# Rotary rows of layer 0's latent heads in blocks of four heads, and where modulation steps, scales and weight slots stand

## The chip, the cores and the metric

One core of one Trainium2 chip. The metric is device microseconds of one execution of the whole program, the median over runs. TensorE (PE) multiplies, VectorE (DVE), ScalarE (ACT) and GpSimd (POOL) do the rest, and SyncE (SP) issues all loads.

## The reference, cut to what matters

Two layers over 256 latent and 256 context tokens of width 1024. Layer 0 mixes tokens by eight heads of window attention with a sink and eight heads of latent attention (MLA); then come 32 experts of which each token uses two. Layer 1 mixes by differential attention, and has 32 experts of its own. All is fp32. The part that the change touches is the latent attention:

```python
q = (_rmsnorm(cq, q_norm) @ w_uq).reshape(b, n, MLA_HEADS, MLA_NOPE_DIM + MLA_ROPE_DIM)
kv = (_rmsnorm(ckv, kv_norm) @ w_ukv).reshape(b, n, MLA_HEADS, MLA_NOPE_DIM + MLA_V_DIM)
...
qr_l = _rope(qr_l, rope_b)
kr_l = _rope(kr_l, rope_b)
...
q = jnp.concatenate([qn, qr], axis=-1)
k = jnp.concatenate([kn, jnp.broadcast_to(kr, kn.shape[:-1] + (MLA_ROPE_DIM,))], axis=-1)
...
s = jnp.einsum('bqhd,bkhd->bhqk', qi, k, preferred_element_type=jnp.float32) * scale
p = jax.nn.softmax(s, axis=-1).astype(v.dtype)
```

A query of a head has 64 plain rows and 32 rotary rows; the 32 rotary rows of the key are shared by all eight heads. Only the latent tokens (the first 256) are rotated. Each layer also needs six modulation vectors, products of the conditioning vectors with a 1024 x 6144 matrix.

## The kernel before, in words

Everything is one program whose order on each engine is the order in which the code is written. A product that must keep fp32 accuracy is made of three fp32r matmuls (`mm3`, L397): each operand is split into a rounded part hi and a rest lo (`split`, L389: a cast on ScalarE at L392, a subtraction at L395 on VectorE or GpSimd), and hi x hi, hi x lo, lo x hi are summed.

Weights flow through one stream in a fixed order (`plan`, `emit`, `pump`, L172) into a pool of 24 slots of 1 MB, shared with data. `budget(n)` says how many slots are kept for data; the next load is issued on SP's queue as soon as fewer weight slots than the rest are held. The order is: input projections, latent up-projections, 19 pieces of modulation weights, four tiles of output projection, five more pieces, the experts of layer 0. Of the experts, the first four are known beforehand; the loads of the others are held back until the ranks of the experts are known (`rank_ids`, L1192, matmuls at L1196; L1199 lifts the limit).

A modulation step (`ada_step`, L317, called by `fill`, L377) multiplies one piece: four fp32 matmuls in four column groups of TensorE (L324). After the eighth step of a vector pair the result is copied (L329), and the next `fill` turns it into place (L359, L364).

Layer 0's attention goes in three stages. **Input projections:** queries, keys and values of the window heads by `mm3`, rotated by `rope_lat` (L566: a product with the cosines at L570, quarter by quarter products with the sines at L573 that swap the halves, a sum at L574); beside them the statistics of the latents, and the shared rotary key (`kr_sum`, L648: a selecting matmul at L650, then `rope_lat`). Four modulation steps lie here.

**Up-projections** (loop at L865, four head pairs): for each head a query matmul group of 128 columns, made of 64 plain rows, 32 rotary rows and zeros (L402 to L404 into psA), a copy (L874), `rope_lat` on rows 64 to 127, and a split. For each pair a key group, whose rows are copied (L890) into a 128-row buffer that holds the rotary key in its lower half (L888), and a split for each head; and a value group, copied at L895. The 16 splits are called through `late` (L657), one behind, with their subtraction on GpSimd. Two modulation steps lie here, and the scores, maxima and exponentials of the first two units (`first`, L861).

**Units** (`run_units`, L776): 24 units of two heads each, numbered as 0 to 7 window heads of latent tokens, 8 to 11 window heads of context tokens, 12 to 19 latent heads of latent tokens, 20 to 23 latent heads of context tokens. Iteration i does, on TensorE: scores of unit i+2 (L688; a mask at L692 for units 0 to 7), the products with the values of unit i-1 (L768), perhaps a modulation step, and the transposes of unit i (L746). On VectorE: the two maxima of unit i+2 (L702) and their negation (L704 with the sink, L708 without), the casts of unit i-1's result (L773, L774), reciprocal and scale of unit i+1 (L733, L737), and one of the two copies of unit i's transposes (L751). On ScalarE: the other copy (L749) and the exponentials of unit i+2 (L720). Window scores have 64 rows a head, so two heads lie in the two halves of TensorE's rows; latent scores have 128 rows a head. `early0` (L908) puts four splits of output weights, 1024 columns each, on GpSimd in iterations 15, 17, 19 and 21.

Then come the output projection (`out_half`, L1563), the router, the ranks, and layer 0's experts.

Of the kernel before, what the change touches and what calls it, by code (L numbers as in the profile page):

```python
# [19 lines left out]
P = 128  # L20
# [22 lines left out]
for _n, _w in (("cosA", 256), ("sinA", 256), ("cosB", 256), ("sinB", 256), ("m0", 128), ("m1", 128), ("U", 128),  # L43
               ("sel", 128)):
    CN[_n] = (_o, _o + _w)
    _o += _w
NCN = _o
NS = 24
KU = 2
# [67 lines left out]
def model_kernel(ctx: ExitStack, tc: tile.TileContext, xin, small, cst, ada0, adaw, win, wuq, wukv, wout0, dwin,  # L117
# [467 lines left out]
    budget(20)  # L585
# [8 lines left out]
    krT = Y.v[:, 3, :]  # L594
    X = S((4, NTOK), F32R)
    Z = S((4, NTOK), F32R)

# [49 lines left out]

    def kr_sum():  # L648
        ps = psB()
        PE.matmul(ps, csv("sel"), krs, start=True, stop=True)  # L650
        ACT.copy(Y.v[64:P, 3, :], ps[64:P, :])
        rope_lat(Y.v[:, 3, :], Y.v[:, 3, :], 64, "cosB", "sinB")
# [19 lines left out]
    def unit_scores(u):  # L672
# [3 lines left out]
        for n in range(1 if lat else 2):  # L676
            q = slice(qt * P, (qt + 1) * P) if lat else slice(SEQ + n * P, SEQ + (n + 1) * P)
            ks = slice(0 if lat else SEQ, NTOK)
            for a, b in ((0, 0), (0, 1), (1, 0)):
                for i in range(2):  # L680
# [3 lines left out]
                    else:  # L684
                        h = 2 * j + i
                        ql, kl = qT[a][h // 4].v[:, h % 4, q], kT[b][h // 4].v[:, h % 4, ks]
                    o = ps[i] if lat else ps[i][:, n * SEQ:(n + 1) * SEQ]
                    PE.matmul(o, ql, kl, start=(a + b == 0), stop=(a == 1 and not masked))  # L688
# [38 lines left out]
    def unit_scale(u, res):  # L727
# [6 lines left out]
        for i in range(2):  # L734
            for n in range(nq):
                w = slice(n * (NTOK // nq), (n + 1) * (NTOK // nq))
                DVE.tensor_scalar(pts[i][:, w], pts[i][:, w], st[:, 0, i, n:n + 1], None, op0=ALU.mult)  # L737
# [107 lines left out]

    wq, wkv = W0.get(), W0.get(False)
    qT = [[S((4, NTOK), F32R) for _ in range(2)] for _ in range(2)]
    kT = [[S((4, NTOK), F32R) for _ in range(2)] for _ in range(2)]
# [10 lines left out]
    kU, ex0 = [], {}  # L859
# [5 lines left out]
    for hp in range(4):  # L865
        for i in range(2):
            h = 2 * hp + i
            if h in (6,99):
                first((6,99).index(h))
            ps = psA()  # L870
            s = slice(h * P, (h + 1) * P)
            mm3(ps, 2, lambda k: (wq[0][:, k, s], wq[1][:, k, s]), lambda k: (X.v[:, k, :], X.v[:, 2 + k, :]))
            dst = U()
            ACT.copy(dst, ps)  # L874
            rope_lat(dst, dst, 64, "cosB", "sinB")
            late(*(x[h // 4].v[:, h % 4, :] for x in qT), dst)
        if hp == 0:
            av_turn()
        if hp in (1,3):
            fill()  # L880
        ps = psB()
        s = slice(hp * P, (hp + 1) * P)
        mm3(ps, 1, lambda k: (wkv[0][:, k, s], wkv[1][:, k, s]), lambda k: kvn3)
        for i in range(2):
            h = 2 * hp + i
            if h < KU:
                kU.append(U())
                DVE.tensor_copy(kU[h][64:P, :], krT[64:P, :])  # L888
            dst = kU[h % KU]
            ACT.copy(dst[0:64, :], ps[64 * i:64 * i + 64, :])  # L890
            late(*(x[h // 4].v[:, h % 4, :] for x in kT), dst)
        ps = psB()
        s = slice(hp * P, (hp + 1) * P)
        mm3(ps, 1, lambda k: (kvn3[0][:, s], kvn3[1][:, s]), lambda k: (wkv[0][:, 0, 512:], wkv[1][:, 0, 512:]))
        DVE.tensor_copy(mv[:, hp, :], ps)  # L895
    split(*lates.pop(0), GP)
    for i in range(2):
        if i not in ex0:
            first(i)
    free(5)  # L900

    oT = [[S((KC, SEQ), F32R) for _ in range(2)]]
    budget(19)
# [4 lines left out]
    def early0(i):  # L908
        if i == 7:
            oT.append([S((KC, SEQ), F32R) for _ in range(2)])  # L910
        if i == 13:
            free(4)
            budget(19)
# [3 lines left out]
    run_units(units, unit_scores, unit_max, unit_exp, unit_scale, unit_transpose, unit_pv, lambda i: True, early0, ex=ex0)  # L917
    fill_all()
    free(9)
# [977 lines left out]
def _constants():  # L1897
# [9 lines left out]
    z = np.zeros((16, SEQ), np.float32)  # L1907
    put("cosB", np.concatenate([z, z, z, z, c.T, z, c.T, z], 0))
    put("sinB", np.concatenate([z, z, z, z, s.T, z, -s.T, z], 0))
# [102 lines left out]
```

## Time and profile before

| | |
|---|---|
| runs | 1484.48, 1480.60, 1483.35 us; median 1483.35 |
| profiled execution | 1484.73 us, its span 1482.6 us |
| TensorE, share of the span | 88% busy, weight loads 49% |
| VectorE, ScalarE, GpSimd | 41%, 26%, 9% |
| DMA | 487 MB, 329 GB/s over the span |

The page cuts the span in 40 slices of 37 us; a digit is a busy share in tenths. In a timeline a row is one instruction or a run of like ones: start, duration of the run, engine, line, operation, output <- input with shapes, count, and in brackets the idle time before it with what ended it. Matmuls overlap, so that the distance from start to start tells what they cost.

### The profile page before, as it was taken

The page shows a single profiled execution, that of the slowest core. Times are in us where ns is not written, and L with a number is a line of the kernel's source. Part 1 is how long each engine was busy: PE and PEld are TensorE (multiplying, and loading weights), DVE is VectorE, ACT ScalarE, POOL GpSimd, SP SyncE. Part 2 cuts the span into 40 slices and gives each one's busy share as a digit, 9 for nine tenths or more (in the row PEclk, how much of TensorE's full clock was granted, in tenths as well). Part 3 has the DMA queues.
Part 4 walks back from the last instruction along what each step waited for, and adds up shares of the span by engine and source line. Part 5 has one row for each costly group of instructions (what it writes and reads, how often), then busy time and mean ns, then how long its engine had stood idle before and what let it go on. Part 6 is the DMA issues. An engine that isn't in the chain of part 4 may idle for free.

```text
span 1482.6 us, 21587 instructions
## 1 busy us (share of the span) xinstructions
PE 1304.1 (88%) x8341; PEld 724.3 (49%) x8341; DVE 602.1 (41%) x1476; ACT 384.5 (26%) x819; POOL 128.0 (9%) x110
## 2 busy tenths in 40 slices
PE   6996999989999999989878999888998787788856
PEld 4673667955445343525326897584442231323313
DVE  4488896453322322222227756944321110111102
ACT  4445655331111110101115333643110010101002
POOL 1134011220000000000013111301000000000000
PEclk9998999999999999999999999999999999998999
DMA  9634715279999999999999228357999999999995
GB/s 382 266 114 152 273 48 211 90 307 374 399 420 422 421 421 420 421 422 420 408 412 382 86 86 304 135 219 276 422 420 422 421 421 420 422 421 421 421 412 228
DMA packets 70075, 487.08 MB, mean 329 GB/s; under 512 B 7632, under 2 KB 7760, under 8 KB 13392
## 3 DMA queue, kind: packets, MB, share of 16 engines
q1 hardware_dynamic: 69968, 485.65, 80.7%
q8 instruction: 68, 1.11, 0.3%
q14 instruction: 39, 0.32, 0.1%
HBM read 484.57 MB, written 1.05 MB: 328 GB/s over the span
## 4 chain that ended last, share of the span: by engine, by line
DMA 25%; PE 16%; DVE 6%; ACT 2%; issue 1%; DVEq 0%; SPq 0%; ACTq 0%
DMA s<-in_ew_dram 25%; PE psA L1336 3%; PE psA L1368 3%; PE psB L403 2%; PE psB L404 2%; PE psB L402 2%; DVE t L1728 1%; DVE u L1746 1%; DVE s L395 1%; PE psA L402 1%; PE psA L403 1%; PE psA L404 1%; PE psB L1385 1%; DVE u L573 0%; DVE s L1378 0%
## 5 line engine op out<-in xcount | busy, mean ns | idle before, releaser
L1336 PE MATMUL psA<-s 128*32 128x512 f32 (+2 forms) x2336 | 418.3, 621 | 81.4 <-DMA s<-in_ew_dram 71.6
L1336 PEld LDWEIGHTS psA<-s 128*32 128x32 f32 (+2 forms) x2336 | 113.7, 122 | 362.7 <-issue 206.2
L1378 DVE SCALAR_TENSOR_TENSOR s<-psB,modT,s 128x256 f32<-128x256 f32 x296 | 120.4, 476 | 215.6 <-PE psB L1385 215.5
L1368 PE MATMUL psA<-s,u 128*32 128x512 f32 (+1 forms) x1168 | 185.9, 601 | 12.8 <-DMA s<-in_ew_dram 11.4
L1373 DVE SCALAR_TENSOR_TENSOR u<-psA,t,u 128x512 fp32r<-128x512 f32 x48 | 36.0, 751 | 233.0 <-ACT u L1372 233.0
L1368 PEld LDWEIGHTS psA<-s,u 128*32 128x32 f32 (+1 forms) x1168 | 53.6, 119 | 123.7 <-issue 95.4
L1510 DVE TENSOR_TENSOR u<-u,psA 128x512 f32<-128x512 f32 x24 | 16.5, 688 | 224.3 <-PE psA L1336 224.3
L1385 PE MATMUL psB<-u 128*128 128x512 f32 (+1 forms) x384 | 95.8, 369 | 13.1 <-DVE s L1378 4.6
L1362 ACT COPY u<-psB 128x512 f32<-128x512 f32 x24 | 14.1, 587 | 332.6 <-PE psB L1360 332.6
L402 PE MATMUL psB<-s 128*128 128x256 f32 (+1 forms) x296 | 96.0, 324 | 3.9 <-DVE s L895 3.9
L403 PE MATMUL psB<-s 128*128 128x256 f32 (+1 forms) x296 | 95.2, 322 | 0.4 <-DVE s L395 0.4
L404 PE MATMUL psB<-s 128*128 128x256 f32 (+1 forms) x296 | 95.1, 321 | 0.0
L1385 PEld LDWEIGHTS psB<-u 128*128 128x128 f32 x384 | 58.7, 188 | 72.1 <-issue 35.7
L1372 ACT ACTIVATE u<-psA,t 128x512 fp32r<-128x512 f32 x48 | 33.0, 688 | 177.2 <-PE psA L1368 171.6
L1507 ACT ACTIVATE u<-psA 128x512 f32<-128x512 f32 x24 | 14.4, 600 | 220.8 <-PE psA L1336 220.8
L1319 PE MATMUL psB<-s 128*128 128x256 f32 x544 | 68.0, 285 | 0.7 <-ACT u L1362 0.7
L395 DVE TENSOR_TENSOR s<-s 128x1024 fp32r<-128x1024 f32 (+3 forms) x56 | 51.6, 967 | 39.9 <-ACT s L392 39.8
L1319 PEld LDWEIGHTS psB<-s 128*128 128x128 f32 x544 | 65.9, 191 | 2.6 <-issue 1.6
L402 PEld LDWEIGHTS psB<-s 128*128 128x128 f32 x296 | 56.4, 190 | 13.8 <-DVE s L895 4.8
L402 PE MATMUL psA<-s 128*128 128x256 f32 (+1 forms) x208 | 62.6, 301 | 0.0
L403 PE MATMUL psA<-s 128*128 128x256 f32 (+1 forms) x208 | 60.5, 291 | 0.0
L404 PE MATMUL psA<-s 128*128 128x256 f32 (+1 forms) x208 | 60.4, 291 | 0.0
(349 smaller groups left out, 1736.6 us busy)
## 6 DMA issues: line engine op xcount, KB each, us to landing
s<-in_ew_dram SPq DMA_DIRECT2D x376, 1024.0 KB, 19.8
s<-in_adaw_dram SPq DMA_DIRECT2D x40, 1024.0 KB, 7.5
s<-in_dwin_dram SPq DMA_DIRECT2D x12, 1024.0 KB, 10.3
s<-in_ada_dram SPq DMA_DIRECT2D x8, 1024.0 KB, 19.8
s<-in_wout_dram SPq DMA_DIRECT2D x8, 1024.0 KB, 7.7
s<-in_ew_dram SPq DMA_DIRECT2D x16, 512.0 KB, 14.4
s<-in_win_dram SPq DMA_DIRECT2D x5, 1024.0 KB, 19.9
s<-in_xin_dram SPq DMA_DIRECT2D x2, 1024.0 KB, 8.6
```

The costliest lines, as they stand in the source:

```text
L395: eng.tensor_tensor(lo, src, hi.bitcast(F32), ALU.subtract)
L402: PE.matmul(ps, lh, rh, start=(k == 0), stop=False)
L403: PE.matmul(ps, lh, rl, start=False, stop=False)
L404: PE.matmul(ps, ll, rh, start=False, stop=(k == n - 1))
L1319: PE.matmul(ps[:, i * n:(i + 1) * n], src(t, cs_(c0 + i)), oh[:, t, 0:n], start=(t == 0 and a == 0), stop=(t == T_ - 1 and a == 1))
L1336: PE.matmul(ps[sl, :], xg(hf * 4 + k, sl), wt(m, hf)[:, k, :], start=(hf == 0 and k == 0), stop=(hf == 1 and k == 3))
L1368: PE.matmul(ps[sl, :], ht[:, k, sl], wt(2, hf)[:, k, :], start=(k == 0), stop=(k == 3))
L1372: ACT.activation(yh, ps, AF.Copy, scale=gsl)
L1373: DVE.scalar_tensor_tensor(out=yl, in0=ps, scalar=gsl, in1=yh.bitcast(F32), op0=ALU.mult, op1=ALU.subtract)
L1378: DVE.scalar_tensor_tensor(out=xc(c)[:, HALF[s]], in0=ps[:, HALF[s]], scalar=modT[:, l, 5, c, s:s + 1], in1=xc(c)[:, HALF[s]], op0=ALU.mul ...
L1385: PE.matmul(ps[:, 0:nt], ysp[a][:, cs_(q)], oht[:, 0:nt], start=(a == 0), stop=(a == 1))
L1510: TT(hm, sl, pm[1], ALU.mult)
```

## The change

The query matrix is reordered: first the 64 plain rows of all heads, two heads to a block of 128, then the rotary rows of four heads to a block, then the same rotary rows with their halves exchanged. Rotary rows are made by two matmul groups, one for each order, and three operations of 128 rows (`rope32`), without the swap of quarters. The rotary key is repeated in four row groups in the same way (`sel`, `sel2`). Plain queries and keys are split straight from PSUM, for two heads at once, the rest on VectorE (`hl_out`). Scores of a latent unit are six matmuls of 64 rows and six of 32 rows. The scale of each unit's second head moves to GpSimd. Modulation steps stand in iterations i with i % 5 in (0, 2, 4), and none in the up-projections but one after them. `budget` keeps fewer slots for data, since the latent heads need six data slots where they needed nine.

```diff
--- before.py
+++ after.py
@@ -41,12 +41,11 @@
 CN = {}
 _o = 0
 for _n, _w in (("cosA", 256), ("sinA", 256), ("cosB", 256), ("sinB", 256), ("m0", 128), ("m1", 128), ("U", 128),
-               ("sel", 128)):
+               ("sel", 128), ("sel2", 128)):
     CN[_n] = (_o, _o + _w)
     _o += _w
 NCN = _o
 NS = 24
-KU = 2
 
 ADL = 3
 
@@ -582,7 +581,7 @@
         return ps
 
 
-    budget(20)
+    budget(17)
     sqs = []
     for j in range(3):
         ACT.copy(Y.v[:, j, :], pss[j])
@@ -591,9 +590,10 @@
         sqs.append(sq)
     sqv = sqs.pop()
     free(3)
-    krT = Y.v[:, 3, :]
     X = S((4, NTOK), F32R)
     Z = S((4, NTOK), F32R)
+
+    kr = [X.v[:, n, :] for n in (0, 2)]
 
     dgs = []
 
@@ -645,11 +645,20 @@
         for s in range(2):
             ACT.activation(krs[:, HALF[s]], pk[:, HALF[s]], AF.Identity, bias=krb[:, s:s + 1])
 
+    def rope32(ps, ps2, dst):
+
+        ACT.copy(dst[:, SEQ:], ps[:, SEQ:])
+        t = U((2, SEQ))
+        DVE.tensor_tensor(t[:, 0, :], ps[:, 0:SEQ], csv("cosB"), ALU.mult)
+        DVE.tensor_tensor(t[:, 1, :], ps2[:, 0:SEQ], csv("sinB"), ALU.mult)
+        DVE.tensor_tensor(dst[:, 0:SEQ], t[:, 0, :], t[:, 1, :], ALU.add)
+
     def kr_sum():
-        ps = psB()
+
+        ps, ps2 = psB(), psA()
         PE.matmul(ps, csv("sel"), krs, start=True, stop=True)
-        ACT.copy(Y.v[64:P, 3, :], ps[64:P, :])
-        rope_lat(Y.v[:, 3, :], Y.v[:, 3, :], 64, "cosB", "sinB")
+        PE.matmul(ps2[:, 0:SEQ], csv("sel2"), krs[:, 0:SEQ], start=True, stop=True)
+        rope32(ps, ps2, Y.v[:, 3, :])
 
     kvn3 = [Z.v[:, n, :] for n in (0, 3)]
     lates, nlate = [], [0]
@@ -682,10 +691,16 @@
                         pr = slice(64 * i, 64 * i + 64)
                         ql, kl = aq[a].v[pr, j, q], ak[b][pr, ks]
                     else:
-                        h = 2 * j + i
-                        ql, kl = qT[a][h // 4].v[:, h % 4, q], kT[b][h // 4].v[:, h % 4, ks]
+                        pr = slice(64 * i, 64 * i + 64)
+                        ql, kl = qn[a].v[pr, j, q], kn[b].v[pr, j, ks]
                     o = ps[i] if lat else ps[i][:, n * SEQ:(n + 1) * SEQ]
-                    PE.matmul(o, ql, kl, start=(a + b == 0), stop=(a == 1 and not masked))
+                    PE.matmul(o, ql, kl, start=(a + b == 0), stop=(a == 1 and kind == "swa" and not masked))
+            for a, b in ((0, 0), (0, 1), (1, 0)) if kind == "mla" else ():
+                for i in range(2):
+                    h = 2 * j + i
+                    pr = slice(32 * (h % 4), 32 * (h % 4) + 32)
+                    o = ps[i] if lat else ps[i][:, n * SEQ:(n + 1) * SEQ]
+                    PE.matmul(o, qr.v[pr, 2 * a + h // 4, q], kr[b][pr, ks], start=False, stop=(a == 1))
         if masked:
             b = (1 - qt) * P
             for i in range(2):
@@ -734,7 +749,11 @@
         for i in range(2):
             for n in range(nq):
                 w = slice(n * (NTOK // nq), (n + 1) * (NTOK // nq))
-                DVE.tensor_scalar(pts[i][:, w], pts[i][:, w], st[:, 0, i, n:n + 1], None, op0=ALU.mult)
+                if i:
+                    GP.tensor_tensor(pts[i][:, w], pts[i][:, w], st[:, 0, i, n:n + 1].to_broadcast([P, NTOK // nq]),
+                                     ALU.mult)
+                else:
+                    DVE.tensor_scalar(pts[i][:, w], pts[i][:, w], st[:, 0, i, n:n + 1], None, op0=ALU.mult)
         return pts
 
     def unit_transpose(u, pts):
@@ -843,9 +862,11 @@
     avt = U()
     ACT.copy(avt, ps)
 
+    split(*lates.pop(0), GP)
     wq, wkv = W0.get(), W0.get(False)
-    qT = [[S((4, NTOK), F32R) for _ in range(2)] for _ in range(2)]
-    kT = [[S((4, NTOK), F32R) for _ in range(2)] for _ in range(2)]
+    qn = [S((4, NTOK), F32R) for _ in range(2)]
+    kn = [S((4, NTOK), F32R) for _ in range(2)]
+    qr = S((4, NTOK), F32R)
     mvB = S((4, NTOK))
     mv = mvB.v
     av = Y.v[:, 0, :].rearrange("p (t n) -> p t n", t=4)
@@ -856,51 +877,50 @@
             PE.transpose(ps[:, t * P:(t + 1) * P], avt[:, t * P:(t + 1) * P], ident)
         ACT.copy(Y.v[:, 0, :], ps)
 
-    kU, ex0 = [], {}
+    ex0 = {}
 
     def first(i):
         u = units[i]
         ex0[i] = unit_exp(u, *unit_max(u, unit_scores(u)))
 
-    for hp in range(4):
-        for i in range(2):
-            h = 2 * hp + i
-            if h in (6,99):
-                first((6,99).index(h))
-            ps = psA()
-            s = slice(h * P, (h + 1) * P)
-            mm3(ps, 2, lambda k: (wq[0][:, k, s], wq[1][:, k, s]), lambda k: (X.v[:, k, :], X.v[:, 2 + k, :]))
-            dst = U()
-            ACT.copy(dst, ps)
-            rope_lat(dst, dst, 64, "cosB", "sinB")
-            late(*(x[h // 4].v[:, h % 4, :] for x in qT), dst)
-        if hp == 0:
+    def hl_out(ps, hi, lo):
+        ACT.copy(hi, ps)
+        DVE.tensor_tensor(lo, ps, hi.bitcast(F32), ALU.subtract)
+
+    def up_q(ps, blk, n):
+        s = slice(blk * P, (blk + 1) * P)
+        mm3(ps[:, 0:n], 2, lambda k: (wq[0][:, k, s], wq[1][:, k, s]),
+            lambda k: (X.v[:, k, 0:n], X.v[:, 2 + k, 0:n]))
+
+    for b in range(2):
+
+        ps, ps2 = psA(), psA()
+        up_q(ps, 4 + b, NTOK)
+        up_q(ps2, 6 + b, SEQ)
+        dst = U()
+        rope32(ps, ps2, dst)
+        split(qr.v[:, b, :], qr.v[:, 2 + b, :], dst, GP)
+        if b == 0:
             av_turn()
-        if hp in (1,3):
-            fill()
-        ps = psB()
-        s = slice(hp * P, (hp + 1) * P)
-        mm3(ps, 1, lambda k: (wkv[0][:, k, s], wkv[1][:, k, s]), lambda k: kvn3)
-        for i in range(2):
-            h = 2 * hp + i
-            if h < KU:
-                kU.append(U())
-                DVE.tensor_copy(kU[h][64:P, :], krT[64:P, :])
-            dst = kU[h % KU]
-            ACT.copy(dst[0:64, :], ps[64 * i:64 * i + 64, :])
-            late(*(x[h // 4].v[:, h % 4, :] for x in kT), dst)
-        ps = psB()
-        s = slice(hp * P, (hp + 1) * P)
-        mm3(ps, 1, lambda k: (kvn3[0][:, s], kvn3[1][:, s]), lambda k: (wkv[0][:, 0, 512:], wkv[1][:, 0, 512:]))
-        DVE.tensor_copy(mv[:, hp, :], ps)
-    split(*lates.pop(0), GP)
-    for i in range(2):
-        if i not in ex0:
-            first(i)
-    free(5)
+        for hp in (2 * b, 2 * b + 1):
+            ps = psB()
+            up_q(ps, hp, NTOK)
+            hl_out(ps, *(x.v[:, hp, :] for x in qn))
+            s = slice(hp * P, (hp + 1) * P)
+            ps = psB()
+            mm3(ps, 1, lambda k: (wkv[0][:, k, s], wkv[1][:, k, s]), lambda k: kvn3)
+            hl_out(ps, *(x.v[:, hp, :] for x in kn))
+            ps = psB()
+            mm3(ps, 1, lambda k: (kvn3[0][:, s], kvn3[1][:, s]),
+                lambda k: (wkv[0][:, 0, 512:], wkv[1][:, 0, 512:]))
+            DVE.tensor_copy(mv[:, hp, :], ps)
+            if hp > 1:
+                first(hp - 2)
+    split(*kr, Y.v[:, 3, :], GP)
+    free(3)
 
     oT = [[S((KC, SEQ), F32R) for _ in range(2)]]
-    budget(19)
+    budget(18)
     fill()
 
     Wo = Splits([(("wout0", j), KC, 2) for j in range(4)])
@@ -909,14 +929,14 @@
         if i == 7:
             oT.append([S((KC, SEQ), F32R) for _ in range(2)])
         if i == 13:
-            free(4)
-            budget(19)
+            free(5)
+            budget(17)
         if i in (15, 17, 19, 21):
             Wo.step(GP)
 
-    run_units(units, unit_scores, unit_max, unit_exp, unit_scale, unit_transpose, unit_pv, lambda i: True, early0, ex=ex0)
+    run_units(units, unit_scores, unit_max, unit_exp, unit_scale, unit_transpose, unit_pv, lambda i: i % 5 in (0, 2, 4), early0, ex=ex0)
     fill_all()
-    free(9)
+    free(7)
     budget(16)
 
 
@@ -1904,15 +1924,15 @@
     put("cosA", np.concatenate([c.T] * 4, 0))
     put("sinA", np.concatenate([s.T, -s.T] * 2, 0))
     c, s = _rope_tables(SEQ, 32)
-    z = np.zeros((16, SEQ), np.float32)
-    put("cosB", np.concatenate([z, z, z, z, c.T, z, c.T, z], 0))
-    put("sinB", np.concatenate([z, z, z, z, s.T, z, -s.T, z], 0))
+    put("cosB", np.concatenate([c.T] * 8, 0))
+    put("sinB", np.concatenate([-s.T, s.T] * 4, 0))
     i = np.arange(P)
     put("m0", np.where(i[None, :] <= i[:, None], 0.0, -1e30))
     put("m1", np.where(i[None, :] >= i[:, None], 0.0, -1e30))
     put("U", (i[:, None] < i[None, :]).astype(np.float32))
 
-    put("sel", (i[None, :] == (64 + 32 * (i % 32 // 16) + i % 16)[:, None]).astype(np.float32))
+    put("sel", (i[None, :] % 32 == i[:, None] % 32).astype(np.float32))
+    put("sel2", (i[None, :] % 32 == (i[:, None] + 16) % 32).astype(np.float32))
     return cst
 
 
@@ -1972,8 +1992,8 @@
     win[4] = kmaj(wi[:, 512:768])
     d["win"] = win
     uq = a["mla_w_uq"][0].reshape(256, 8, 96)
-    z = np.zeros((256, 8, 16), f)
-    d["wuq"] = kmaj(np.concatenate([uq[..., :80], z, uq[..., 80:], z], -1).reshape(256, 1024))
+    d["wuq"] = kmaj(np.concatenate([x.reshape(256, -1) for x in (
+        uq[..., :64], uq[..., 64:], np.concatenate([uq[..., 80:], uq[..., 64:80]], -1))], 1))
     kv = a["mla_w_ukv"][0].reshape(P, 8, 128)
     d["wukv"] = np.concatenate([kv[..., :64].reshape(P, 512), kv[..., 64:].reshape(P, 512)], 1)
     wo = a["ab_w_out"][0]
```

## Rows read from the trace of the kernel before

**Rows 1.** The page: its head, slices of 37 us, chain of waits.

```profile
span 1482.6 us, 21587 instructions
...
DMA  9634715279999999999999228357999999999995
...
DMA 25%; PE 16%; DVE 6%; ACT 2%; issue 1%; DVEq 0%; SPq 0%; ACTq 0%
```

**Rows 2.** Timeline of TensorE at the ranks of layer 0's experts.

```profile
323.95 0.40 PE L1196 MATMUL psB<-u,sm 32*128 32x32 f32 x2
```

**Rows 3.** Timeline of TensorE: up-projections, transposes of units 0, 1, 12, 20, output projection.

```profile
99.00 0.39 PE L402 MATMUL psA<-s 128*128 128x512 f32 x1
99.23 0.39 PE L403 MATMUL psA<-s 128*128 128x512 f32 x1
...
138.69 1.97 PE L746 MATMUL psB<-identR,u 128*128 128x128 f32 x8 [6.58 <-DVE u L737]
...
145.67 1.09 PE L746 MATMUL psB<-identR,u 128*128 128x128 f32 x8
...
191.25 1.09 PE L746 MATMUL psB<-identR,u 128*128 128x128 f32 x8
...
226.69 1.97 PE L746 MATMUL psB<-identR,u 128*128 128x128 f32 x8
...
240.45 0.39 PE L402 MATMUL psA<-s 128*128 128x256 f32 x1
```

**Rows 4.** Groups by line and form, 120 to 330 us: count, busy us, mean ns.

```profile
L720 ACT ACTIVATE u<-psA,t 128x512 f32<-128x512 f32 x32 | 21.9, 689 | 3.1 <-DVE t L708 2.6 <-DVE t L704 0.4
...
L702 DVE TENSOR_REDUCE t<-psA 128x1 f32<-128x512 f32 x32 | 20.5, 683 | 4.2 <-PE psA L688 2.5 <-PE psA L692 1.7
...
L395 POOL TENSOR_TENSOR s<-u,s 128x512 fp32r<-128x512 f32 x9 | 12.2, 1375 | 7.5 <-ACT s L392 7.5
...
L392 ACT CAST s<-u 128x512 fp32r<-128x512 f32 x8 | 4.9, 620 | 7.5 <-DVE u L574 7.5
```

**Rows 5.** Timeline of TensorE: a window unit with a step, a latent unit.

```profile
153.98 1.09 PE L746 MATMUL psB<-identR,u 128*128 128x128 f32 x8
155.00 0.98 PE L688 MATMUL psA<-s 64*128 64x512 f32 x6
155.91 0.28 PE L692 MATMUL psA<-s 128*128 128x128 bf16 x2
156.12 1.09 PE L768 MATMUL psB<-u,s 128*64 128x128 f32 x16
157.15 1.07 PE L324 MATMUL psC<-s,scS 128*32 128x512 f32 x8
158.15 1.09 PE L746 MATMUL psB<-identR,u 128*128 128x128 f32 x8
...
195.89 1.64 PE L688 MATMUL psA<-s 128*128 128x512 f32 x6
197.46 1.16 PE L768 MATMUL psB<-u,s 128*64 128x128 f32 x16
198.54 1.09 PE L746 MATMUL psB<-identR,u 128*128 128x128 f32 x8
```

**Rows 6.** Timeline of VectorE and GpSimd in a window unit and in latent units.

```profile
156.18 1.29 DVE L702 TENSOR_REDUCE t<-psA 128x1 f32<-128x512 f32 x2 [0.37 <-PE psA L692]
...
198.70 0.17 DVE L708 TENSOR_SCALAR t<-t 128x2 f32<-128x2 f32 x1
...
202.18 2.39 POOL L395 TENSOR_TENSOR s<-s 128x1024 fp32r<-128x1024 f32 x1 [63.83 <-PE psB L768]
202.21 2.39 DVE L708 TENSOR_SCALAR t<-t 128x2 f32<-128x2 f32 x1
...
205.03 0.15 DVE L733 RECIPROCAL t<-t 128x2 f32<-128x2 f32 x1
205.22 0.88 DVE L737 TENSOR_SCALAR u<-u,t 128x512 f32<-128x512 f32 x2
```

## The prediction

> **What bounds the kernel now.** I read the page first, then the timelines of the stretch that the diff edits, engine by engine. The page [rows 1] shows DMA at 9 tenths or more through layer 0's experts (slices 9 to 21) and again from slice 28 on, and the chain of waits is made of expert loads for a quarter of the span. Between lie compute stages. The diff edits one of them, from the latent up-projections to the last attention unit of layer 0. What is saved there is saved for good only if the expert stream behind it starts earlier too. The loads of the unranked experts may be issued only after the ranks are known, by two small matmuls at 323.95 [rows 2]; these wait for output projection and router, which wait for the attention. I take it that a shift of the attention's end shifts all that follows by as much.
>
> In the stretch I mark three points [rows 3]: the first up-projection matmul at 99.00, the transposes of unit 0, T(0), at 138.69, and the first matmul of the output projection at 240.45. From 99.00 to 138.69 are 39.7 us, in which TensorE's matmuls, one per 0.227 us (99.00 to 99.23), need only some 20; T(0) itself waited 6.58 us for VectorE and then took 1.97 for its eight transposes, against 1.09 later [rows 5]. VectorE and GpSimd are the bound there: 16 head splits on GpSimd at 1.375 us [rows 4], beside rotary additions on VectorE that stall behind them.
>
> The units, 138.69 to 240.45, run in iterations on TensorE: scores of unit i+2, values of unit i-1, perhaps a modulation step, transposes of unit i. A window unit with a step [rows 5]: T 1.02, scores of 64 rows 0.91, mask 0.21, values 1.03, step 1.00, in all 4.17, TensorE without a gap, while VectorE idles 0.37 [rows 6]. A latent unit without a step [rows 5]: scores 1.57, values 1.08, then T, and VectorE takes 3.51 from one negation to the next with no wait [rows 6].
>
> **The change part by part.** The parts follow the program's order; the sum is made against the profiled execution, 1484.73 us (span 1482.6 and 2.1 around it), which stands 1.4 above the median 1483.35.
>
> *Rotary key.* A second selecting matmul of 256 columns in plain fp32. Four such of 512 columns side by side take a step's 1.00 [rows 5], so half the columns cost 0.5, on a TensorE that is full there: +0.5. Its three VectorE operations replace four; nothing.
>
> *Up-projections.* Gone are 48 query matmuls of 512 columns, 32 rotary operations on single heads, 2 copies and the 16 splits on GpSimd. New: 36 query matmuls of 512 columns and 12 of 256, two rotary blocks (copy, three operations, one split each), and per head pair two copies on ScalarE and two subtractions on VectorE. TensorE then has 2 x 2.05 for the blocks, 4 x 2.72 for the pairs (12 matmuls at 0.227), 0.5 for turning the window values (half a T), 2 x 1.12 for the first two units' scores: 17.7. I follow the queues. From 99.5, with one wait of 0.6 for a bank, scores of unit 0 end at 114.0. VectorE's two maxima at 0.683 [rows 4] and the negation end at 115.6. ScalarE then has unit 0's exponentials: two of 0.689 [rows 4], by my estimate 1.7 with their small companions, to 117.4, and the last pair's two copies queue behind them, to 118.6. VectorE's three operations on that pair, of the size of a maximum, end at 119.9, unit 1's maximum at 121.4, its exponentials at 123.1. Now comes the rotary key's split, its cast at 0.620 [rows 4] to 123.7 and its subtraction on GpSimd to 125.1; behind it in GpSimd's queue stands the new scale of unit 0's second head, to 126.4, and only then can T(0) finish. TensorE has idled since about 120.5, so I let it run as slowly as after T(0)'s wait before, when the way to T(1) took 6.98 [rows 3]. Less the step and the modulation turn that are not there now (1.6) and the first half of T(0) (0.95), 4.4 remain: T(1) at about 130.8 instead of 145.67. **Gain 14.9**, the +0.5 inside. Bounds: T(1) at 126 if the key's split waits for nobody, at 134 if VectorE and GpSimd collide as before.
>
> *Scores of the latent units.* Six matmuls of 128 rows become six of 64 rows and six of 32. The 64-row six cost 0.91 [rows 5], two heads side by side. No row shows 32-row pairs. Lower end: three pairs at 0.227 with no wait at the change, 0.68; upper end: one after the other, six at 0.227 and 0.2, 1.57. I take 0.91, since the 64-row pairs are nearest: two heads in different row groups, writing different banks. The latent iteration then is 1.82 + 1.03 + 1.02 = 3.87 on TensorE, 0.37 more than before, and TensorE is its bound.
>
> *Second head's scale to GpSimd.* It takes 0.4 from VectorE's queue in each unit (two heads take 0.88, from 205.22 [rows 6]): a window iteration without a step becomes 4.17 - 0.37 - 0.4 = 3.40, a latent one 3.10. GpSimd's product has no row; the subtraction of that size has 1.375 [rows 4] and the one of double size 2.39 [rows 6]. I take 1.375. It is wanted by the second half of T one iteration later, about 0.8 after it is done: nothing. At 2.39 that half would wait 0.3, over 22 units 6.6 us.
>
> The place where this can hurt is the four splits of the output weights on GpSimd. There VectorE's 2-element negation takes 2.39 us instead of 0.17, from 202.21, just as long as GpSimd's subtraction from 202.18 [rows 6]. GpSimd's new product queues behind that subtraction, and VectorE may wait again. Part of it is hidden by the longer TensorE iterations, three of which have a modulation step; I take 0.9 for each of the four that is not. The Trainium skill (SBUF — State Buffer, Who interferes with whom) states that VectorE, in a two-port mode or with two SBUF inputs, and GpSimd exclude each other for the whole instruction, and that who comes first wins. The trace agrees, 2.39 against 2.39; by that rule alone every unit's new product could hold up VectorE, which is the first rival below.
>
> *Modulation steps.* Before, 7 ahead of the units and 12 in units 0 to 11; now 5 ahead and 14 over units 0 to 22. A step is 1.00 where TensorE bounds and less elsewhere. Iterations 2 to 12 become 4.17, 3.40, 4.17, 4.77, 3.40, 3.97, 3.5, 3.97, 4.87, 3.87, 4.87 = 45.0 (the 0.6 more in the fourth is a modulation turn), against 191.25 - 145.67 = 45.6. Iterations 13 to 20: 8 x 3.87, five steps, a turn and three stalls, 39.3, against 226.69 - 191.25 = 35.4. The rest: 3.87, 3.05, 2.05, about 3 for the end and a stall, 13, against 13.8 [rows 3]. **Loss 2.5.**
>
> *More weight slots.* Their loads arrive in a stretch where DMA is 1 to 7 tenths busy (slices 1 to 7 [rows 1]), and no unit waits for them. The steps free their slots later, so output weights are issued later, one slot for each step; the first is wanted in unit 15, after 13 steps, and seven slots admit it then. Nothing, as long as a load lands within two units, 9 us. SP's queue carries the same loads.
>
> Sum: 14.9 - 2.5 = 12.4 of gain; 1484.7 - 12.4 = 1472.3, and for a median, which stands 1.4 lower, about 1471.
>
> **The rivals.** (1) *GpSimd takes the port first.* Its product and VectorE's scale of the first head are released by the same reciprocal. If GpSimd wins, VectorE waits 1.375 in each unit: window iterations without a step go from 3.40 to 4.78 (three, 4.1), those with one gain 0.6 (1.2 for two), three around the context units 2.5, five latent ones without a step 3.0 (3.10 + 1.375 against 3.87), the four with output weights 5.5, the last two 2.8: 19 us, so 1490, slower. It decides from about 0.9 us per unit on, where 12 us are used up. For it: the stalls of [rows 6]. Against: VectorE starts its scale 0.04 us after its own reciprocal (205.03 and 0.15, then 205.22), and a signal to another engine is hardly quicker. (2) *The 32-row matmuls run one after the other.* 1.57 instead of 0.91 in twelve units, 7.9: 1479. For it: no row shows a pair. Against: the 64-row pairs. (3) *The gain is hidden.* If the expert stream were paced from before the ranks, an earlier attention would only wait longer: 1483. For it: DMA's share of the chain [rows 1]. Against: the stream's limit is released by the ranks [rows 2].
>
> **How the numbers follow.** Forecast 0.75, rival (1) 0.09, (2) 0.11, (3) 0.05. Within 0.3%, about what a measurement of this kernel can tell from no change, means 1478.9 to 1487.8. The forecast lies below that almost wholly (0.74), (2) astride its lower end (0.04 below), (1) at or over its upper end (0.06 over). Faster 0.78, same 0.16, slower 0.06. The range goes down to 1463 (T(1) at 126, less 4.8, and 32-row pairs at 0.68, less 2.8) and up to 1480, which takes in (2) and, of the forecast, a slower product on GpSimd.
>
> **What would show it.** Right: T(1) near 131; latent iterations near 3.9 and 4.9 with TensorE gapless; two heads' 32-row matmuls starting together; VectorE's scale still 0.44; ranks and all behind them 12 us earlier at the same distances. Wrong: VectorE's scale at 1.4 or more in ordinary units, latent scores over 2.3, or TensorE waiting for GpSimd's products at every T; or ranks earlier, but the experts' end unmoved.

## The result and the profile after

The changed kernel takes 1471.6 us (median, 1470.3 to 1473.7) against 1482.0 for the kernel before beside it (1480.5 to 1484.5): ratio 0.993, 95% interval 0.9908 to 0.9951, so 10.4 us or 0.7% less. The forecast was about 1471. The profiled execution of the changed kernel took 1473.68, its span 1471.9.

The page of the changed kernel, its head, slices and chain, beside [rows 1]:

```profile
span 1471.9 us, 21790 instructions
...
DMA  9834444489999999999998238356999999999995
...
DMA 26%; PE 16%; DVE 7%; ACT 2%; issue 1%; DVEq 0%; SPq 0%; ACTq 0%
```

The picture is the old one: DMA is full but for slices 1 to 8 and 22 to 27. TensorE's timeline of the changed kernel has the same marks as [rows 3] and [rows 2]: first up-projection, T(0) in two halves, T(1), T(12), T(20), output projection, ranks.

```profile
98.06 0.39 PE L401 MATMUL psA<-s 128*128 128x512 f32 x1
...
120.94 0.66 PE L765 MATMUL psB<-identR,u 128*128 128x128 f32 x4 [1.16 <-DVE u L756]
125.06 1.12 PE L765 MATMUL psB<-identR,u 128*128 128x128 f32 x4 [3.47 <-POOL u L753]
...
129.92 1.75 PE L765 MATMUL psB<-identR,u 128*128 128x128 f32 x8
...
175.44 1.09 PE L765 MATMUL psB<-identR,u 128*128 128x128 f32 x8
...
214.05 1.09 PE L765 MATMUL psB<-identR,u 128*128 128x128 f32 x8
...
229.04 0.39 PE L401 MATMUL psA<-s 128*128 128x256 f32 x1
...
312.56 0.40 PE L1216 MATMUL psB<-u,sm 32*128 32x32 f32 x2
```

I call **A** the way from the first up-projection to T(1), **B** that from T(1) to the output projection. A fell from 46.67 to 31.86, B rose from 94.78 to 99.12; the start came 0.94 earlier. Together the ranks are 11.39 earlier (312.56 against 323.95), and from them to the end there is as much as before, 1159.3 against 1158.6.

### The profile page after: what moved, and what is told of

Same layout as the page of the kernel before. It is cut to its first block, busy times and chain, and to the rows that moved or that the text cites. A ratio compares the mean times of both kernels' runs of the same rounds, so it can differ in the third digit from the quotient of the medians.

```text
span 1471.9 us, 21790 instructions
## 1 busy us (share of the span) xinstructions
PE 1306.0 (89%) x8439; PEld 720.9 (49%) x8439; DVE 578.9 (39%) x1423; ACT 373.1 (25%) x800; POOL 139.6 (9%) x129
## 4 chain that ended last, share of the span: by engine, by line
DMA 26%; PE 16%; DVE 7%; ACT 2%; issue 1%; DVEq 0%; SPq 0%; ACTq 0%
DMA s<-in_ew_dram 26%; PE psA L1356 3%; PE psA L1388 2%; PE psB L402 2%; PE psB L403 2%; PE psB L401 2%; DVE t L1748 1%; DVE u L1766 1%; PE psA L401 1%; PE psA L402 1%; PE psA L403 1%; DVE s L394 1%; DVE u L572 0%; DVE t L1764 0%; DVE s L1398 0%
## 5 line engine op out<-in xcount | busy, mean ns | idle before, releaser
L1388 PE MATMUL psA<-s,u 128*32 128x512 f32 (+1 forms) x1168 | 186.9, 606 | 11.7 <-DMA s<-in_ew_dram 10.4
L401 PE MATMUL psB<-s 128*128 128x256 f32 (+1 forms) x304 | 98.8, 325 | 0.2 <-DVE s L888 0.2
L402 PE MATMUL psB<-s 128*128 128x256 f32 (+1 forms) x304 | 98.1, 323 | 0.3 <-DVE s L394 0.3
L403 PE MATMUL psB<-s 128*128 128x256 f32 (+1 forms) x304 | 98.0, 322 | 0.0
L1339 PEld LDWEIGHTS psB<-s 128*128 128x128 f32 x544 | 65.9, 191 | 2.6 <-issue 1.6
L401 PEld LDWEIGHTS psB<-s 128*128 128x128 f32 x304 | 57.9, 190 | 8.4 <-issue 1.7
L402 PEld LDWEIGHTS psB<-s 128*128 128x128 f32 x304 | 57.9, 190 | 4.7 <-DVE s L394 0.6
L403 PEld LDWEIGHTS psB<-s 128*128 128x128 f32 x304 | 57.9, 190 | 4.5
L401 PE MATMUL psA<-s 128*128 128x256 f32 (+1 forms) x200 | 58.7, 294 | 0.0
```

Of the source, the lines that this page charges most:

```text
L401: PE.matmul(ps, lh, rh, start=(k == 0), stop=False)
L402: PE.matmul(ps, lh, rl, start=False, stop=False)
L403: PE.matmul(ps, ll, rh, start=False, stop=(k == n - 1))
L1339: PE.matmul(ps[:, i * n:(i + 1) * n], src(t, cs_(c0 + i)), oh[:, t, 0:n], start=(t == 0 and a == 0), stop=(t == T_ - 1 and a == 1))
L1388: PE.matmul(ps[sl, :], ht[:, k, sl], wt(2, hf)[:, k, :], start=(k == 0), stop=(k == 3))
```

## Experiments

Each run is compared with the kernel before on the same chip (its median was 1482.56 beside the key's split later, the steps as before, the layout alone and the first run with the scaling on VectorE; 1483.38 beside the slots and the three runs below them in the table; 1481.13 beside the second runs and the last two). In the profiled executions the start of A lies between 95.28 and 99.47, although nothing ahead of it but the weight slots differs among the changed kernel and its variants. A and B are the sharper measure, though each comes from one execution: the changed kernel run again gave 31.87 and 99.07.

| kernel | median us | ratio (95%) | A | B | A + B |
|---|---|---|---|---|---|
| before | 1481.1 to 1483.4 | 1 | 46.67 | 94.78 | 141.45 |
| changed | 1471.6 | 0.993 (0.9908 to 0.9951) | 31.86 | 99.12 | 130.98 |
| changed, again | 1472.0 | 0.9929 (0.9911 to 0.9947) | 31.87 | 99.07 | 130.94 |
| scaling on VectorE | 1471.2 | 0.9926 (0.9907 to 0.9944) | 28.58 | 99.02 | 127.60 |
| the same, again | 1470.0 | 0.9913 (0.9896 to 0.993) | 28.56 | 99.01 | 127.57 |
| key's split later | 1466.8 | 0.99 (0.9883 to 0.9917) | 26.69 | 99.43 | 126.12 |
| steps as before | 1478.8 | 0.9973 (0.9959 to 0.9986) | 34.95 | 103.27 | 138.22 |
| layout alone | 1472.4 | 0.9931 (0.9915 to 0.9948) | 32.85 | 98.66 | 131.51 |
| slots as before | 1473.1 | 0.9937 (0.992 to 0.9954) | 31.79 | 99.14 | 130.93 |
| key later, scaling on VectorE | 1469.4 | 0.9907 (0.9889 to 0.9924) | 27.47 | 99.27 | 126.74 |
| key later, two steps ahead | 1467.4 | 0.9898 (0.9881 to 0.9915) | 26.69 | 99.42 | 126.11 |
| query matmuls twice | 1476.1 | 0.9955 (0.9939 to 0.9971) | 34.37 | 99.08 | 133.45 |
| steps as before, output weights on VectorE | 1470.8 | 0.992 (0.9901 to 0.9938) | 34.77 | 94.72 | 129.49 |
| key later, output weights on VectorE | 1465.5 | 0.988 (0.986 to 0.9899) | 26.69 | 97.46 | 124.15 |

**Which part carries the gain: the layout alone.** Scaling, steps and slots as before the change:

```diff
-                if i:
-                    GP.tensor_tensor(pts[i][:, w], pts[i][:, w], st[:, 0, i, n:n + 1].to_broadcast([P, NTOK // nq]),
-                                     ALU.mult)
-                else:
-                    DVE.tensor_scalar(pts[i][:, w], pts[i][:, w], st[:, 0, i, n:n + 1], None, op0=ALU.mult)
+                DVE.tensor_scalar(pts[i][:, w], pts[i][:, w], st[:, 0, i, n:n + 1], None, op0=ALU.mult)
...
+            if hp in (1, 3):
+                fill()
...
-lambda i: i % 5 in (0, 2, 4)
+lambda i: True
```

(and budgets of 20, 19 and 19.)

> The new layout of heads and rotary rows alone: scaling on VectorE, steps and weight slots as before the change. Theory: the layout carries the whole gain; T(1) 4 us earlier than in the changed kernel since nothing waits for GpSimd, steps about -1, and the window iterations have a step each (4.1 to 4.2), which hides VectorE's 3.4. About 1467. Rival (the other three parts carry half of the gain or more): 1476 or above.

1472.4: the whole gain is there, so the other three parts together bring nothing that can be measured. But it isn't 1467: A is 32.85, longer than the changed kernel's. Three more steps stand in it, two in the up-projections and that of iteration 1 just ahead of T(1). And something does wait for GpSimd: a two-element addition of VectorE takes 1.24 beside the rotary key's difference (123.55 beside 123.47, 1.30), TensorE waits 1.70 for VectorE behind it and runs on at a granted clock of 0.67 (126.56 to 131.80). The theory that the parts add up fails; the next runs show how they interact.

**Scaling on VectorE** (the first hunk above), and the same again beside the changed kernel:

> Both heads' scalings on VectorE again, all else as in the changed kernel (1471.6). Theory (the gain lies in the up-projection stage, and the units are bound by TensorE): transposes T(0) no longer wait for GpSimd, which had the rotary key's difference first (second half of T(0) at 125.06), so T(1) starts some 4 us earlier than 129.92; VectorE then has 3.4 of work in a window unit against TensorE's 3.17, so the five iterations without a step lose 0.23 each, 1.2 in all; latent iterations stay at 3.84 and 4.83. Sum -2.8: about 1469. Rival (taking the scaling off VectorE carries the gain): 0.4 more in each of 24 units, about 1481.

> Both heads' scalings on VectorE, as in the first experiment, beside the changed kernel on the same chip. Theory (by the traces, in which the stretch from the up-projections to the out projection is 3.4 shorter): 3 less than the run beside it. Rival (by the medians of the first comparison): within 1 of it.

> The changed kernel unchanged, beside the next one on the same chip: 1471 to 1473.

A is 3.3 shorter. B is the same, but made of two parts: T(1) to T(20) is 0.8 longer (84.96 against 84.13), of the 1.2 expected, and T(20) to the output projection 0.9 shorter (14.06 against 14.99). The medians say 0.4 less in the first comparison and 2.0 less beside the changed kernel; their intervals overlap, so the times settle nothing and confirm neither theory's number. By the traces, which agree in both runs, GpSimd's scaling costs 3.4 of A + B here; it does not gain.

**Rotary key's split later:**

```diff
-    split(*kr, Y.v[:, 3, :], GP)
     free(3)
...
     def early0(i):
+        if i == 2:
+            split(*kr, Y.v[:, 3, :], GP)
```

> The split of the rotary key (a ScalarE cast, a GpSimd difference of 1.26) stands in iteration 2 of the units instead of just ahead of them; all else as in the changed kernel. Theory: GpSimd scales unit 0's second head as soon as VectorE has the reciprocal, at about 121, so the second half of T(0) starts near 122.2 and not at 125.06, T(1) near 126 and not at 129.92; iteration 2 has room on ScalarE and GpSimd. Sum -3 to -4: about 1468. Rival (T(0) and T(1) wait for the maxima and exponentials of unit 1 on VectorE and ScalarE anyway): 1471 to 1472.

Confirmed: 1466.8. In the changed kernel the chain ahead of T(0) is the one in the prediction; ScalarE, GpSimd and VectorE there:

```profile
121.83 0.61 ACT L391 CAST s<-s 128x512 fp32r<-128x512 f32 x1
...
122.57 1.26 POOL L394 TENSOR_TENSOR s<-s 128x512 fp32r<-128x512 f32 x1 [10.67 <-DVE t L748]
123.79 2.22 POOL L753 TENSOR_TENSOR u<-u,t 128x512 f32<-128x512 f32 x2
...
122.58 1.53 DVE L756 TENSOR_SCALAR u<-u,t 128x512 f32<-128x512 f32 x1
```

The product that the second half of T(0) needs (123.79) stands behind the key's difference (122.57), for which the cast on ScalarE (121.83) was late. VectorE's scaling of the next unit, 1.53 instead of 0.49, lies beside the same difference. With the split moved, GpSimd and TensorE do this:

```profile
120.30 1.32 POOL L753 TENSOR_TENSOR u<-u,t 128x512 f32<-128x512 f32 x1 [8.58 <-DVE t L748]
...
121.67 0.66 PE L765 MATMUL psB<-identR,u 128*128 128x128 f32 x4 [0.24 <-POOL u L753]
124.58 1.09 PE L765 MATMUL psB<-identR,u 128*128 128x128 f32 x8
```

The wait is 0.24 instead of 3.47, and T(1) takes 1.09 instead of 1.75. The length of T(1) is the clock's doing: the changed kernel's windows of 5 us have

```profile
core 0: us, PE busy (x) PEld busy (x) DVE busy (x) ACT busy (x) POOL busy (x), PEclk, DMA share, GB/s
...
121.00:126.00 5.00, 1.53 (x8) 1.07 (x8) 3.01 (x6) 3.64 (x12) 3.43 (x3) 0.85 0.71 283
126.00:131.00 5.00, 5.00 (x30) 3.62 (x30) 2.96 (x8) 0.00 (x0) 0.01 (x1) 0.50 0.00 2
```

a granted clock of 0.50 (the lower of the two levels) after TensorE had been busy for only 1.53 of 5. With the split moved, TensorE is busy 4.76 of the same 5 (121 to 126), and the granted clock is 1.00 there and in the next 5. **Key later and scaling on VectorE:**

> The rotary key's split in iteration 2 and both heads' scaling on VectorE. Theory: with both scalings on VectorE T(1) started at 127.1, and 1.1 of that was VectorE's two-element add held for 1.26 beside GpSimd's difference, so T(1) comes near 126 (124.6 with the scaling split and the key later); after that the units took 99.0 with VectorE's scaling and 99.4 with the split one. Sum +1 against the kernel with the key later alone (1466.8): 1467 to 1469. Rival (GpSimd's scaling costs more, through the port, than it gives): 1465 or less.

1469.4 against 1466.8, as expected within the intervals (A + B: 0.6 more). So GpSimd's scaling is worth some 0.6 once nothing stands ahead of it in GpSimd's queue, and costs 3.4 where the key's split does. **Two steps ahead of the units** (with the key later):

```diff
-    fill()
+    fill(2)
...
-lambda i: i % 5 in (0, 2, 4)
+lambda i: i % 5 in (0, 2, 4) and i != 2
```

> The rotary key's split in iteration 2, and two modulation steps instead of one ahead of the units (iteration 2 has none). Theory: the second step's 1.07 of TensorE falls into the 1.17 in which TensorE waits for VectorE ahead of T(0), and iteration 2 is 0.97 shorter: about 1466, at best 1465.5. Rival (the step's copy on ScalarE and its transposes delay T(0) or T(1) by as much): 1467 or above.

No difference: the step itself was free (A 26.69 both times), but iteration 2, shorter by it, only made the next one longer: T(1) to T(2) 4.3 and T(2) to T(3) 4.6, where without the edit they are 5.3 and 3.6. The rival's time came, but not for its reason. In that kernel without the edit VectorE is busy 18.9 of the 20 us from 118 on, so it, not TensorE, is the likely pace there; no run isolated that.

**Slots as before:**

> The weight slots as before the change (budgets 20, 19, 19), all else as in the changed kernel. Theory: the slots are worth nothing, since no matmul of the stages concerned waits for a weight in either trace: T(1) at 130, out projection at 229, 1471 to 1472. Rival (more slots let the DMA run ahead and are part of the gain): 1475 or above, with TensorE waits that a DMA ends.

Nothing: A and B are within 0.07, and the median, 1473.1, is 1.1 to 1.5 above the two of the changed kernel, within the intervals.

**Query matmuls twice:**

```diff
-            up_q(ps, hp, NTOK)
+            for _ in range(2):
+                up_q(ps, hp, NTOK)
```

> The changed kernel, with the up-projection of each pair's 64-row query heads made twice into the same bank (the second starts afresh, so the values are the same): four times six matmuls of 0.23, 5.5 of TensorE, about what the change took out of the stage. Theory: the change's gain in that stage had two parts, TensorE's 5.4 and the splits and rotary operations on GpSimd, VectorE and ScalarE that held it; TensorE is now the bound up to unit 1's scores (busy 22.1 of 27), so T(1) comes 4.5 to 5.5 later, 1476 to 1477, and two thirds of the 15.7 stay. Rival (the stage is still paced by VectorE and ScalarE): the extra matmuls lie beside them, T(1) at most 2 later, 1473 or less.

The medians say 4.1 to 4.5 more, and 1476.1 lies in the theory's range, but the profiled execution (the shortest of the twelve) has A only 2.5 longer. Counted from the start of A, the second unit's scores come 5.2 later (22.65 instead of 17.42), and the second half of T(0) 3.8 later (30.83 instead of 27.00): TensorE's wait for VectorE ahead of T(0), 1.16 in the changed kernel, is gone. From there to T(1) it takes 3.54 instead of 4.86, at a granted clock of 0.76 instead of 0.50. So the clock gave 1.3 back in that execution; whether it did so in the others, no trace shows. By any of these numbers TensorE's matmuls were at most a third of the 14.8, and this is an upper bound: the layout itself took only some 1.3 of query matmuls away (48 at 0.227 against 36 at 0.227 and 12 at 0.117), and two modulation steps, 2.1, moved out of the stage. The larger part is the work taken off GpSimd, VectorE and ScalarE; no run tells the three apart. The windows from the first up-projection to T(0), first of the kernel before, then of the changed one to its second half:

```profile
99.00:138.70 39.70, 27.54 (x134) 16.59 (x132) 31.90 (x52) 23.34 (x48) 23.06 (x17) 0.93 0.42 159
```

```profile
98.06:125.00 26.94, 22.13 (x121) 15.20 (x119) 16.55 (x33) 14.07 (x35) 6.30 (x6) 0.99 0.37 136
```

(the columns are those above: PE, PEld, DVE, ACT, POOL). GpSimd 23.1 to 6.3, VectorE 31.9 to 16.6, TensorE 27.5 to 22.1. Part of VectorE's 31.9 is time in which GpSimd held it. One of its rotary additions in the kernel before with GpSimd idle, then one beside a difference of GpSimd:

```profile
120.88 0.42 DVE L574 TENSOR_TENSOR u<-u 64x256 f32<-64x256 f32 x1
...
122.61 1.32 DVE L574 TENSOR_TENSOR u<-u 64x256 f32<-64x256 f32 x1
```

```profile
122.09 1.56 POOL L395 TENSOR_TENSOR s<-u,s 128x512 fp32r<-128x512 f32 x1 [2.03 <-ACT s L392]
```

The 32 rotary operations of the eight heads took 22.7 in all, and would have taken 13.5 at the 0.42 to 0.43 that each takes alone: 9.2 was time held (an estimate from these rows). The six of the changed kernel take 0.41 or 0.42 each.

**Steps as before:**

> The modulation steps where they stood before the change (after pairs 1 and 3, one ahead of the units, then in each of iterations 0 to 11); all else as in the changed kernel. Theory: a step costs TensorE 0.97 wherever TensorE is the bound, so it only moves: five more in the windows +4.9, seven fewer in the later units -6.8, one of the two in the up-projections +1.0, the other lies in TensorE's idle time ahead of T(0). Latent iterations all 3.84. Sum about -1: 1470 to 1472. Rival (the spread of the steps carries part of the gain): 1476 to 1479.

The theory falls, and the rival's time comes: 1478.8, B 103.27 instead of 99.12 and A 3.1 longer (three more steps stand in it). Eight latent iterations at TensorE's 3.84 are 30.7, and T(12) to T(20) takes 39.6. Its GpSimd, VectorE and TensorE at the first split of the output weights:

```profile
191.93 2.38 POOL L394 TENSOR_TENSOR s<-s 128x1024 fp32r<-128x1024 f32 x1 [0.95 <-ACT s L391]
...
192.53 1.79 DVE L723 TENSOR_SCALAR t<-t 128x2 f32<-128x2 f32 x1
...
197.04 1.97 PE L787 MATMUL psB<-u,s 128*64 128x128 f32 x14 [1.64 <-DVE u L770]
198.94 1.71 PE L765 MATMUL psB<-identR,u 128*128 128x128 f32 x8
```

VectorE's negation of two elements ends with GpSimd's difference, everything on VectorE comes late, TensorE waits 1.64, and then runs at a granted clock of 0.56 (197.04 to 200.65). New theory: it is this stall, and spreading the steps pays because a step gives TensorE work while VectorE catches up. The test moves the four differences:

```diff
-            Wo.step(GP)
+            Wo.step(DVE)
```

> The kernel with the modulation steps as before the change (1478.8), and the four differences of the output weights' splits on VectorE instead of GpSimd. Theory, formed from its trace: there the latent units took 39.6 for eight iterations of 3.84 (30.7), since each GpSimd difference of 2.36 held VectorE's next small operation (1.64 to 1.79 instead of 0.17), TensorE ran dry behind it and then ran at the slow clock; with the differences on VectorE (about 1.1 each) no operation is held, T(12) to T(20) comes to 32 to 35 and T(20) to the out projection to 15 instead of 17: 1471 to 1474. Rival (the steps' absence itself, or the DMA, makes the stalls): T(12) to T(20) stays above 38, 1477 or above.

> The rotary key's split in iteration 2 and the output weights' differences on VectorE, the steps spread. Theory: here the spread steps cover most of what the differences hold, and TensorE idles only 0.7 to 2 of it: T(12) to T(20) 36 to 38 instead of 38.6, so 1465 to 1467 against 1466.8. Rival (the differences' 1.1 on VectorE are late where VectorE is the bound): 1468 or above.

Confirmed: with the steps as before, B falls by 8.5, to 94.72, T(12) to T(20) from 39.6 to 34.6, and the median by 8.0. VectorE there, where it was held:

```profile
193.20 0.17 DVE L723 TENSOR_SCALAR t<-t 128x2 f32<-128x2 f32 x1
193.31 1.23 DVE L394 TENSOR_TENSOR s<-s 128x1024 fp32r<-128x1024 f32 x1
```

The negation takes 0.17, the difference 1.23 instead of 2.38. The windows of T(12) to T(20) and on to the output projection, first with the differences on GpSimd, then on VectorE:

```profile
179.90:219.50 39.60, 35.98 (x326) 26.26 (x324) 33.73 (x67) 19.56 (x51) 16.46 (x12) 0.93 0.02 7
219.50:236.50 17.00, 14.53 (x90) 9.11 (x89) 11.03 (x20) 10.21 (x27) 6.05 (x7) 0.86 0.48 186
```

```profile
180.60:215.10 34.50, 33.44 (x326) 24.27 (x324) 30.60 (x69) 19.25 (x51) 9.78 (x9) 1.00 0.02 7
215.10:228.60 13.50, 12.30 (x89) 7.53 (x88) 8.92 (x23) 9.92 (x27) 4.14 (x6) 1.00 0.61 234
```

The granted clock is 1.00 again in both. With the steps spread and the key's split moved the same edit is worth 2.0 of B, and T(12) to T(20) is 37.8, as expected. That kernel takes 1465.5, ratio 0.988 (0.986 to 0.9899): the best version here, 6.5 below the changed kernel beside it.

## Why the prediction was right, point by point

**The stage of the up-projections** was right in mechanism and size. From the start to the second half of T(0) the text has 99.5 to 126.4, 26.9; the trace has 27.0. From there to T(1) it has 4.4, the trace 4.86, at the slow clock as assumed. The chain of steps (exponentials, copies, key's cast, key's difference, product) is the measured one, and moving its one avoidable link gave an A of 26.69, the lower bound of the text (99.5 to 126, 26.5). The reading of the stage before holds too, and its stalls on VectorE are the 9.2 above; only TensorE was busier there than the text has it, 27.5 and not some 20. The start was 0.94 earlier instead of 0.5 later; the starts of the variants scatter by 4.2, so nothing of the change, the 0.5 of the rotary key included, is read from that. Layout alone shortens A by 13.8.

**Latent units.** Taken: scores 1.82, iterations 3.87 and 4.87 with TensorE gapless. TensorE in a latent unit of the changed kernel, beside [rows 5]:

```profile
176.46 0.98 PE L697 MATMUL psA<-s 64*128 64x512 f32 x6
177.37 0.96 PE L703 MATMUL psA<-s 32*128 32x512 f32 x6
178.26 1.09 PE L787 MATMUL psB<-u,s 128*64 128x128 f32 x16
```

The six of 32 rows take 0.89, from 177.37 to 178.26, so two heads run side by side; rival (2), 1.57, is out. Iterations are 3.84 and 4.83. What was missed is the context units: four groups of six, of 256 columns, cost 0.55 each, 2.2 in place of 1.82 (and of 1.6 before):

```profile
198.87 0.62 PE L697 MATMUL psA<-s 64*128 64x256 f32 x6
199.42 0.62 PE L703 MATMUL psA<-s 32*128 32x256 f32 x6
199.97 0.62 PE L697 MATMUL psA<-s 64*128 64x256 f32 x6
200.52 0.62 PE L703 MATMUL psA<-s 32*128 32x256 f32 x6
201.07 1.09 PE L787 MATMUL psB<-u,s 128*64 128x128 f32 x16
```

**The sum over the units.** T(1) to T(12): 45.52, taken 45.0. T(12) to T(20): 38.61, taken 39.3. The rest: 14.99, taken 13; one context unit's scores, the last split's stall and the end are longer. So the units lost 4.3 where 2.5 was taken. In the forecast A and B together gained 12.9, and the start cost 0.5: 12.4. Measured are 10.5 and a start 0.9 earlier: 11.4 at the ranks. That the total comes so near is in part luck, since the start made up for 1.4 of the 2.4 by which A and B fell short. The median's nearness, 1471.6 to 1471, is in part luck too: the forecast counted its 12.4 from a median of 1483.35, the measured 10.4 counts from 1482.0.

**GpSimd's product** takes 1.04 alone, not 1.375. The reason given against rival (1), that a signal to another engine is hardly quicker than VectorE's own next instruction, is right by the start times, but does not decide who goes first. VectorE and GpSimd in four latent iterations, beside [rows 6]:

```profile
172.16 1.36 DVE L756 TENSOR_SCALAR u<-u,t 128x512 f32<-128x512 f32 x1
175.98 1.36 DVE L756 TENSOR_SCALAR u<-u,t 128x512 f32<-128x512 f32 x1
180.55 0.49 DVE L756 TENSOR_SCALAR u<-u,t 128x512 f32<-128x512 f32 x1
184.38 0.48 DVE L756 TENSOR_SCALAR u<-u,t 128x512 f32<-128x512 f32 x1
```

```profile
172.19 1.04 POOL L753 TENSOR_TENSOR u<-u,t 128x512 f32<-128x512 f32 x1 [3.21 <-DVE t L748]
176.02 1.04 POOL L753 TENSOR_TENSOR u<-u,t 128x512 f32<-128x512 f32 x1 [2.78 <-DVE t L748]
180.61 1.32 POOL L753 TENSOR_TENSOR u<-u,t 128x512 f32<-128x512 f32 x1 [3.55 <-DVE t L748]
184.44 1.32 POOL L753 TENSOR_TENSOR u<-u,t 128x512 f32<-128x512 f32 x1 [2.51 <-DVE t L748]
```

In two of the four GpSimd's product went first, and VectorE's scaling waited for it. Of the 16 scalings of 512 columns two have no such race, since GpSimd was busy with the key's difference; three of the other fourteen were lost so. In all fourteen GpSimd's product starts after VectorE's scaling in the record: by 0.03 to 0.04 where GpSimd went first, by 0.06 to 0.14 where VectorE did. So it is no chance: the same three units lost in the second run of the changed kernel. What kept the rival's 19 us away is that GpSimd wins seldom, and that latent iterations bound by TensorE leave VectorE room; T(1) to T(20) is even 0.8 shorter than with both scalings on VectorE. The other sign named for it, TensorE waiting for GpSimd's product at every T, was seen at T(0) alone. The Trainium skill (SBUF — State Buffer, Who interferes with whom) has it that whoever issues first holds the port pair that the two share for the whole instruction; the trace agrees that one waits out the other, in both directions, 1.36 against 1.04 and 0.49 against 1.32. That the first to issue wins it does not show: by the recorded starts VectorE is first in all fourteen.

**The output weights' splits.** 0.9 was taken for four times, 3.6; moving them to VectorE gains, net of its own work, 2.0 in B with the steps spread, and 8.5 with the steps as before. So the largest thing that the prediction did not see is that the change's parts lean on one another: GpSimd's scaling costs 6.7 of A + B beside the old steps (138.22 against 131.51, where the slots are the old ones too, which were worth nothing), and spreading the steps gives 7.2 back, 3.09 of it in A, which three steps leave, and 4.15 in B, which they enter. Spread steps were costed as merely moved.

**Rivals (2) and (3)** are out: the pairs run side by side, and the 11.39 at the ranks went through to the end, 0.7 of it lost on the way. **The slots** are worth nothing, as taken.

## What to carry to other kernels

A stage paced by three engines gives back more than TensorE's share when a layout takes work off all of them; follow the queues to find which single late link then ends it, and look whether that link has to stand there. Before moving an operation to GpSimd, list what already stands in its queue and which of VectorE's instructions it can hold; a two-element operation that took 1.79 instead of 0.17 cost TensorE a wait of 1.64 and then its clock. Filler work is worth most beside such a stall (7.2 here), and little once the stall is gone: with the differences on VectorE some 0.5, an estimate (A + B 129.49 with the steps as before, and 124.15 plus the 4.9 of the key's split with the steps spread).

## What the runs showed of the hardware

- Which of VectorE and GpSimd goes first, when one reciprocal releases both, is not always the same: VectorE in eleven scalings of 512 columns, GpSimd's product in three. In all nine profiles of kernels that scale on GpSimd, GpSimd went first wherever its recorded start lay 0.03 to 0.04 behind VectorE's, and VectorE first from 0.06 on; whether that lag is the cause, no run shows.
- A difference of 128x1024 takes GpSimd 2.35 to 2.38 and VectorE 1.22 to 1.23. Beside it on GpSimd, VectorE's next small operation took 1.64 to 2.29 instead of 0.17 (steps as before), so that VectorE was held for longer than the difference would have cost it.
- After TensorE had been busy 1.53 of 5 us, the next 5 us had a granted clock of 0.50, and eight transposes took 1.75 instead of 1.09.
